# Narrow experts multiply the loaded float32 weights as they are, two products side by side in the halves of the array's columns

## The chip, the cores and the metric

The kernel runs on one core of one Trainium2 chip, as one program. The metric is the device time of an execution in microseconds. TensorE (PE; PEld are its weight loads) multiplies into PSUM, VectorE (DVE) and ScalarE (ACT) work between PSUM and SBUF, and SyncE (SP) issues nearly all transfers from memory.

## The reference

A network of four layers for 256 tokens and a width of 1024, in float32: a retention layer with a dense feed-forward part, a banded attention layer with a mixture of experts, and two layers of a second kind with a feed-forward part of 4096. The change touches only the mixture of experts:

```python
logits = (xn @ w_router).astype(jnp.float32)
top_v, top_i = lax.top_k(logits, 2)
top_w = jax.nn.softmax(top_v, axis=-1)
gates = jnp.sum(one_hot(top_i, 8) * top_w[..., None], axis=-2)
for e in range(8):
    y = y + gates[..., e:e + 1] * ((silu(xn @ w_gate[e]) * (xn @ w_up[e])) @ w_down[e])
```

Here w_gate and w_up are 1024 x 3584 for each expert and w_down is 3584 x 1024.

## The kernel before, in words

**Split products.** A float32 operand is split into a high part (ScalarE rounds it to the type fp32r) and a low part (VectorE subtracts the high part from the operand). A full product is three fp32r products: high x high, high x low and low x high (mm3, lines 343 to 345).

**The stream of weights.** All weights lie packed in the order of their use, in chunks of 128 partitions x 2048 numbers (1 MiB). The class Stream loads them with one transfer each, in that order, into places: 4 in the pool raw, 3 and 4 more in raw3 and raw4 that widen adds late in the attention layer for the time of the experts. _split makes the two parts of half a chunk (whi on line 288, wlo on line 289), and get asks for splits up to 5 half chunks ahead (HL). When the second half is split the place is free, and fill issues the next transfer into it (line 267).

**Turns of experts.** After the routing, the experts are put in an order by how many tokens chose them, and are worked on in eight turns. WIDE says which turns have 128 slots for tokens and which have 64: turns 1, 4 and 7 are narrow. gather picks the tokens of an expert by a product with a one-hot matrix oh and splits them. A wide turn has them as xgh and xgl and uses mm3. In a narrow turn the high part stands in the first 64 of 128 columns and the low part in the other 64, so that one product of 128 columns gives both; it is done with whi and with wlo (lines 1033 and 1034), and the two halves of the result have to be added.

**One step.** An expert has 14 steps j of 256 hidden columns. A step has two up chunks, with gate and up columns (8 blocks of 128 rows, 512 columns), and one down chunk (2 blocks of 128 rows, 1024 columns). In a narrow turn ScalarE copies the 512 result columns from PSUM (cp, line 1064), four products with the matrix fold (line 1069) turn them and add the two halves, ScalarE makes the silu (sgn, line 1073), VectorE multiplies (line 1074), and the result hh is split (lines 348 and 349) for the down products, which add to two PSUM banks acc. The down products of step j - 1 come after the up products of step j. At the end acc is split into yh and yl, a product with the one-hot matrix ohT brings the rows back to their tokens (line 1112), and VectorE adds them to h by their gates (line 1114).

**Order.** The planner of the language orders each engine's instructions by priority and by when they become ready in its own model; each engine then runs them in that order. Waits are derived from what is read and written. A wide turn has 24 up and 12 down products per step, a narrow one 16 and 8, and four with fold.

Of the kernel before, what the change touches and what calls it, by code (L numbers as in the profile page):

```python
# [227 lines left out]
class Stream:  # L228


    def __init__(self, prog, plans, raw_bufs, hl_bufs, raw_pool, hl_pool):
        self.nc = prog.nc
        self.items, self.parts, self.first = [], [], []
        for ap, plan in plans:
            offs, _ = offsets(plan)
            for c, o in zip(plan, offs):
                self.first.append(len(self.parts))
                step = max(c.kt // 2, 1)
                self.parts += [(len(self.items), k, step) for k in range(0, c.kt, step)]
# [3 lines left out]
        self.free = {raw_pool: raw_bufs}  # L243
        self.base, self.extra = raw_pool, []
# [4 lines left out]
    def widen(self, pool, bufs, until):  # L249

        self.extra.append(pool)
        self.free[pool] = bufs
        self.last = next(i for i, it in enumerate(self.items) if it[1].key == until)
        self.fill()

    def fill(self, most=None):
        while self.n_raw < min(len(self.items), most or len(self.items)):
            pool = next((p for p in self.extra if self.n_raw <= self.last and self.free[p]), self.base)
            if not self.free[pool]:
                return  # L260
            ap, c, o = self.items[self.n_raw]
            f = c.kt * c.n
            t = pool.tile([P, 2048], F32, name="wraw")
            if c.key[0] in ("eu", "ed"):
                e = self.expert[c.key[1]] if c.key[1] else 0
                src = ap[e:e + 1] if isinstance(e, int) else ap[bass.ds(e, 1)]
                self.nc.sync.dma_start(t[:, :f], src[:, o:o + P * f].rearrange("o (p f) -> (o p) f", p=P))
            else:
                step = f if self.n_raw else f // 2
                for c0 in range(0, f, step):  # L270
                    self.nc.sync.dma_start(t[:, c0:c0 + step],
                                           bass.AP(tensor=ap.tensor, offset=ap.offset + o + c0, ap=[[f, P], [1, step]]))
            self.free[pool] -= 1
            self.raw[self.n_raw] = t, pool
            self.n_raw += 1

    def _split(self):
        i, k, nk = self.parts[self.n_hl]
        c = self.items[i][1]
        self.fill()  # L280
        t, pool = self.raw[i]
        f = nk * c.n
        hi, lo = (self.hl_pool.tile([P, 1024], F32R, name=n) for n in ("whi", "wlo"))
        n = 1 if c.key[0] in ("eu", "ed") and c.key[1] < NE - 1 else 2
        for i0 in range(0, f, f // n):
            h, l = (x[:, i0:i0 + f // n] for x in (hi, lo))
            src = t[:, k * c.n + i0:k * c.n + i0 + f // n]
            self.nc.scalar.activation(h, src, AF.Copy)  # L288
            self.nc.vector.tensor_tensor(l, src, h.bitcast(F32), op=ALU.subtract)  # L289
        if k + nk == c.kt:  # L290
            self.free[pool] += 1
            del self.raw[i]
        self.hl[self.n_hl] = [x[:, :f].rearrange("p (k n) -> p k n", n=c.n) for x in (hi, lo)]
        self.n_hl += 1
        self.fill()

    def get(self, *keys):

        at = self.first[self.n_get]
# [3 lines left out]
        end = self.first[self.n_get]  # L303
        while self.n_hl < min(max(end, at + self.hl_bufs), len(self.parts)):
            self._split()
        return [[x[:, k, :] for x in self.hl[i]] for i in range(at, end) for k in range(self.parts[i][2])]


class Program:
# [200 lines left out]
    def run(self):  # L510
        nc, io = self.nc, self.io
        self.we = io["we"].rearrange("(e f) -> e f", e=NE)
        with ExitStack() as st, ExitStack() as self.later, \
                ExitStack() as self.routed, ExitStack() as self.wide:
            pool = self.lasting = lambda *a, **kw: st.enter_context(self.pool(*a, **kw))
            raw_pool, hl_pool = pool("raw", self.RAW), pool("hl", self.HL)
# [6 lines left out]
                            raw_pool, hl_pool)  # L523
# [279 lines left out]
    def widen(self, name, bufs):  # L803

        self.w.widen(self.wide.enter_context(self.pool(name, bufs)), bufs, ("ed", NE - 1, FFE // 256 - 1))
# [171 lines left out]
    def gather(self, px, pool, slot, turns, wide):  # L977
# [12 lines left out]
        xg = (px.tile([P, KD, n, P], F32R, name="xgh"), px.tile([P, KD, n, P], F32R, name="xgl"))  # L990
        for k2 in range(KD // 2):
            ks = slice(2 * k2, 2 * k2 + 2)
            ps = self.bank("ps")[:, :2 * n * P].rearrange("p (k e s) -> p k e s", k=2, e=n)
            for k in range(2):
                at = 0
                for x in self.xn:
                    for b in range(NB):
                        nc.tensor.matmul(ps[:, k], x[:, b, (2 * k2 + k) * P:(2 * k2 + k + 1) * P],
                                         oh[:, b], start=at == 0, stop=at == 3)
                        at += 1  # L1000
# [3 lines left out]
            flat = lambda t: t.rearrange("p k e s -> p k (e s)")  # L1004
            cut = nw * P + 64
            nc.scalar.activation(flat(xg[0][:, ks])[:, :, :cut], flat(ps)[:, :, :cut], AF.Copy)
            if nw:
                nc.vector.tensor_tensor(xg[1][:, ks, 0], ps[:, :, 0], xg[0][:, ks, 0].bitcast(F32), op=ALU.subtract)
            nc.vector.tensor_tensor(xg[0][:, ks, nw, 64:], ps[:, :, nw, 64:], xg[0][:, ks, nw, :64].bitcast(F32), op=ALU.subtract)
# [6 lines left out]
        return {i: ([x[:, :, a] for x in (xg if wide[i] else xg[:1])], ohT[:, a]) for a, i in enumerate(turns)}  # L1016

    def experts(self, px, pool, gates, slot, w, first, wide):
# [5 lines left out]
        for e in range(NE):  # L1024
            xg, ohT = have[e]
            acc = [self.bank("acc") for _ in range(2)]
            hT = {}

            def product(out, x, wk, start, stop):
                if wide[e]:  # L1030
                    self.mm3(out, x, wk, start, stop)
# [8 lines left out]
            def down(rows, by_half=False):  # L1040
                order = [(n, r) for n in range(2) for r in rows] if by_half else [(n, r) for r in rows for n in range(2)]
                for n, (j, k, wk) in order:
                    product(acc[n], [a[:, k, :] for a in hT[j]], [a[:, n * 512:(n + 1) * 512] for a in wk],
                            j == 0 and k == 0, j == nj - 1 and k == 1)

            def turned(j, ps):


                hh = pool.tile([P, 2, P], F32R, name="hh", bufs=2)
                if wide[e]:  # L1050
                    sg = self.work.tile([P, 256], F32, name="sg", tag="xs", bufs=3)
# [10 lines left out]
                hT[j] = (hh,)  # L1062
                cp = self.work.tile([P, 512], F32, name="cp", tag="xs", bufs=3)
                nc.scalar.activation(cp, ps, AF.Copy)

                def turn():
                    tp = self.bank("tp")[:, :256].rearrange("p (c s) -> p c s", s=64)
                    for c in range(4):
                        nc.tensor.matmul(tp[:, c], cp[:, c * P:(c + 1) * P], self.fold, start=True, stop=True)

                    def split():
                        sg = self.work.tile([P, 2, 64], F32, name="sgn", tag="xs", bufs=3)
                        nc.scalar.activation(sg, tp[:, :2], AF.Silu)
                        nc.vector.tensor_tensor(sg, sg, tp[:, 2:], op=ALU.mult)
                        self.split_psum(hh[:, :, :64], hh[:, :, 64:], sg)
# [4 lines left out]
            for j in range(nj):  # L1080
                ps = self.bank("mm")
                for k0 in (0, 4):
# [4 lines left out]
                    for k in range(4):  # L1087
                        product(ps, [a[:, k0 + k, :] for a in xg], wu[k],
                                k0 + k == 0, k0 + k == KD - 1)
# [13 lines left out]
            with self.tc.high_priority(offset=300) if e == NE - 1 else nullcontext():  # L1103
                for n in range(2):
                    spare = n and e == NE - 1
                    y = (pool.tile([P, 512], F32R, name="yh", bufs=2),
                         px.tile([P, 512], F32R, name="yl", tag="xgl") if spare else pool.tile([P, 512], F32R, name="yl"))
                    self.split_psum(*y, acc[n])
                    for b in range(NB):
                        ps = self.bank("ps")  # L1110
                        for i in range(2):
                            nc.tensor.matmul(ps, ohT[:, b * P:(b + 1) * P], y[i], start=i == 0, stop=i == 1)
                        s = self.h[:, b, n * 512:(n + 1) * 512]
                        nc.vector.scalar_tensor_tensor(s, ps, gates[:, b, e:e + 1], s, op0=ALU.mult, op1=ALU.add)

    def moe_layer(self):
# [19 lines left out]
        with tc.If(most > P):  # L1136
            with self.pool("moe2") as pool, self.pool("raw2", 2) as raw, \
# [495 lines left out]
```

## Time and profile before

| | us |
|---|---|
| median of 3 runs (2431.17 to 2432.93) | 2431.45 |
| profiled execution | 2430.9 |
| its span | 2429.1 |

The mean granted TensorE clock is 0.993 of full speed. The span is the time from the first to the last instruction in the trace. Busy times of TensorE are those of overlapping, pipelined products, so the distance between the starts of two products says more than a product's duration.

### The profile page before, as it was taken

What the parts mean: (1) busy time and instruction counts of PE and PEld (TensorE: products, weight loads), DVE (VectorE), ACT (ScalarE), POOL (GpSimd) and SP (SyncE); (2) the same over time, 40 slices, a digit from 0 to 9 for tenths busy, and PEclk for the clock granted to TensorE, in tenths of its full rate; (3) what the DMA queues carried; (4) which work ended last, traced back from release to release, by engine and by line L of the source; (5) the groups of instructions that cost most, each with busy time, mean ns of one, the idle gap of its engine ahead of it and who ended that gap; (6) DMA issues with size and microseconds to landing.
All of it is one profiled execution on the core that took longest, in us unless ns stands there. A gap on an engine that the chain in (4) does not pass through costs nothing. (4 is left out here: it accounts for less than half of the span.)

```text
span 2429.1 us, 35661 instructions
## 1 busy us (share of the span) xinstructions
PE 2372.9 (98%) x13033; PEld 1968.2 (81%) x13033; DVE 1891.5 (78%) x3027; ACT 1568.7 (65%) x2609; POOL 60.5 (2%) x105
## 2 busy tenths in 40 slices
PE   8999999999999999999999999899999999999999
PEld 7978998888876787876788876698789889878898
DVE  6756567778989989899998899778775567877655
ACT  6446555667878777778777789645755554575554
POOL 0000000000000000000000000100000000100000
PEclk9999999999999999999999999899999999999999
DMA  7445555567989998999999999534345554434552
GB/s 289 169 161 209 190 191 191 203 239 283 368 327 399 360 366 330 356 356 413 345 366 345 367 359 381 148 134 160 137 165 203 188 168 145 169 128 173 191 191 105
DMA packets 88121, 605.20 MB, mean 249 GB/s; under 512 B 10456, under 2 KB 12128, under 8 KB 17024
## 3 DMA queue, kind: packets, MB, share of 16 engines
q1 hardware_dynamic: 85520, 593.39, 65.5%
q0 software_dynamic: 2416, 9.44, 1.8%
q8 instruction: 104, 1.70, 0.3%
q14 instruction: 81, 0.66, 0.1%
HBM read 601.74 MB, written 1.05 MB: 248 GB/s over the span
## 5 line engine op out<-in xcount | busy, mean ns | idle before, releaser
L289 DVE TENSOR_TENSOR wlo<-wraw,whi 128x512 fp32r<-128x512 f32 (+1 forms) x1656 | 1383.5, 876 | 369.6 <-ACT whi L288 351.7
L288 ACT ACTIVATE whi<-wraw 128x512 fp32r<-128x512 f32 (+1 forms) x1656 | 1204.1, 776 | 437.0 <-PE mm L344 191.6
L343 PE MATMUL mm<-xth,whi 128*128 128x256 f32 x1296 | 364.0, 281 | 0.0
L345 PE MATMUL mm<-xth,wlo 128*128 128x256 f32 x1296 | 361.7, 279 | 1.5 <-DVE wlo L289 1.5
L344 PE MATMUL mm<-xtl,whi 128*128 128x256 f32 x1296 | 361.8, 279 | 0.0
L344 PEld LDWEIGHTS mm<-xtl,whi 128*128 128x128 f32 x1296 | 245.5, 189 | 3.9 <-issue 2.1
L343 PEld LDWEIGHTS mm<-xth,whi 128*128 128x128 f32 x1296 | 243.5, 188 | 5.2 <-issue 3.0
L344 PE MATMUL acc<-wlo,hh 128*128 128x512 f32 x624 | 247.2, 396 | 0.0
L345 PE MATMUL acc<-whi,hl 128*128 128x512 f32 x624 | 246.6, 396 | 0.0
L345 PEld LDWEIGHTS mm<-xth,wlo 128*128 128x128 f32 x1296 | 243.6, 188 | 2.4 <-DVE wlo L289 1.7
L343 PE MATMUL acc<-whi,hh 128*128 128x512 f32 x624 | 235.3, 397 | 1.3 <-ACT hh L348 1.3
L343 PE MATMUL mm<-whi,xth 128*128 128x512 f32 (+2 forms) x592 | 231.3, 391 | 2.0 <-ACT whi L288 2.0
L344 PE MATMUL mm<-wlo,xth 128*128 128x512 f32 (+2 forms) x592 | 231.5, 391 | 0.3 <-DVE wlo L289 0.3
L345 PE MATMUL mm<-whi,xtl 128*128 128x512 f32 (+2 forms) x592 | 229.6, 388 | 0.5 <-DVE xtl L349 0.5
L343 PE MATMUL mm<-whi,xgh 128*128 128x512 f32 x560 | 224.9, 402 | 2.7 <-ACT whi L288 2.6
L344 PE MATMUL mm<-wlo,xgh 128*128 128x512 f32 x560 | 223.0, 398 | 3.1 <-DVE wlo L289 3.0
L345 PE MATMUL mm<-whi,xgl 128*128 128x512 f32 x560 | 221.4, 395 | 0.0
L1034 PE MATMUL mm<-wlo,xgh 128*128 128x512 f32 x336 | 143.3, 427 | 5.4 <-DVE wlo L289 4.5
L343 PEld LDWEIGHTS acc<-whi,hh 128*128 128x128 f32 x624 | 117.5, 188 | 28.9 <-ACT hh L348 3.2
L345 PEld LDWEIGHTS acc<-whi,hl 128*128 128x128 f32 x624 | 117.3, 188 | 28.2 <-DVE hl L349 0.5
L344 PEld LDWEIGHTS acc<-wlo,hh 128*128 128x128 f32 x624 | 117.4, 188 | 26.4 <-DVE wlo L289 0.3
L1033 PE MATMUL mm<-whi,xgh 128*128 128x512 f32 x336 | 134.2, 400 | 0.0
(394 smaller groups left out, 3098.0 us busy)
## 6 DMA issues: line engine op xcount, KB each, us to landing
wraw<-in_we_dram SPq DMA_DIRECT2D x336, 1024.0 KB, 6.1
wraw<-in_w_dram SPq DMA_DIRECT2D x218, 1024.0 KB, 4.8
wraw<-in_w_dram SPq DMA_DIRECT2D x4, 912.0 KB, 4.6
wraw<-in_w_dram SPq DMA_DIRECT2D x6, 512.0 KB, 3.6
bias<-in_rel_rows_dram POOLq DMA_DIRECT2D x4, 768.0 KB, 4.6
gain<-in_norm_ffn_dram POOLq DMA_DIRECT2D x2, 512.0 KB, 7.1
gn<-in_ret_gn_dram SPq DMA_DIRECT2D x4, 256.0 KB, 3.8
gain<-in_norm_ple_dram POOLq DMA_DIRECT2D x2, 512.0 KB, 5.9
```

Of the source, the lines that this page charges most:

```text
L288: self.nc.scalar.activation(h, src, AF.Copy)
L289: self.nc.vector.tensor_tensor(l, src, h.bitcast(F32), op=ALU.subtract)
L343: mm(out, l[0], r[0], start=start, stop=False)
L344: mm(out, l[0], r[1], start=False, stop=False)
L345: mm(out, l[1], r[0], start=False, stop=stop)
L1033: nc.tensor.matmul(out, x[0], wk[0], start=start, stop=False)
L1034: nc.tensor.matmul(out, x[0], wk[1], start=False, stop=stop)
```

## The change

Stream takes a list of plain turns (1, 4 and 7). Their chunks get no parts: get hands out the loaded float32 numbers themselves, keeps the chunk in held, and frees its place at the next get. The places are now parts of one tile per pool (4, 3 and 4 places), handed out in the order in which they become free. Splits ahead are only asked for if the chunk's transfer has been issued.

gather makes xn, the 64 slots of a narrow expert in full float32, in place of the two parts side by side. The new helper halves multiplies 64 slots by two column halves of a weight block, into partitions 0 to 63 and 64 to 127 of one PSUM bank, one product after the other in program order. The up result is 256 columns wide (gate in the upper half, up in the lower half), two transposes take the place of the fold products, and the product of silu and up goes to hn in float32 with no split. The down result fits one bank; its rows are brought back to the tokens by products over 64 rows each.

```diff
     def get(self, *keys):
+        for i in self.held:
+            self.release(i)
...
+        while self.n_hl < min(max(end, at + self.hl_bufs), len(self.parts)) \
+                and (self.n_hl < end or self.parts[self.n_hl][0] in self.raw):
             self._split()
+        if not self.plain(self.items[start][1]):
+            return [[x[:, k, :] for x in self.hl[i]] for i in range(at, end) for k in range(self.parts[i][2])]
+        self.held = list(range(start, self.n_get))
+        return [[t[:, a, k * c.n:(k + 1) * c.n]] for i in self.held
+                for (t, a), c in [(self.raw[i], self.items[i][1])] for k in range(c.kt)]
...
+    def room(self, pool, n, last):
+        t = pool.tile([P, n, 2048], F32, name="wraw")
+        self.last[id(t)] = last
+        self.free += [(t, k) for k in range(n)]
...
+    def halves(self, out, xs, ws, first, last):
+        m, width = None, out.shape[1]
+        for i, (x, (w,)) in enumerate(zip(xs, ws)):
+            for n in range(2):
+                before = [m] if m else []
+                m = self.nc.tensor.matmul(out[64 * n:64 * n + 64], x, w[:, n * width:(n + 1) * width],
+                                          start=first and i == 0, stop=last and i == len(xs) - 1)
+                self.after(m, before)
+        return m
...
-                    nc.tensor.matmul(out, x[0], wk[0], start=start, stop=False)
-                    nc.tensor.matmul(out, x[0], wk[1], start=False, stop=stop)
+                    self.halves(ps[:, :256], [xg[:, k0 + k, :] for k in range(4)], wu, k0 == 0, k0 + 4 == KD)
...
+                if not wide[e]:
+                    if rows:
+                        ends.append(self.halves(acc[0], [hT[j][:, k, :] for j, k, _ in rows], [wk for *_, wk in rows],
+                                                 rows[0][:2] == (0, 0), rows[-1][:2] == (nj - 1, 1)))
+                    return
...
-                cp = self.work.tile([P, 512], F32, name="cp", tag="xs", bufs=3)
-                nc.scalar.activation(cp, ps, AF.Copy)
+                hT[j] = pool.tile([P, 2, 64], F32, name="hn", tag="hh", bufs=2)
+                cp = self.work.tile([P, 256], F32, name="cp", tag="xs", bufs=3)
+                nc.scalar.activation(cp, ps[:, :256], AF.Copy)
...
-                    for c in range(4):
-                        nc.tensor.matmul(tp[:, c], cp[:, c * P:(c + 1) * P], self.fold, start=True, stop=True)
+                    for k in range(2):
+                        self.after(nc.tensor.transpose(tp[:, k], cp[:, k * P:(k + 1) * P], self.ident), ends[-1:])
...
-                        self.split_psum(hh[:, :, :64], hh[:, :, 64:], sg)
+                        nc.vector.tensor_tensor(hT[j], sg, tp[:, :, 64:], op=ALU.mult)
```

## Rows read from the trace of the kernel before

**Rows 1.** The page: busy time, share and instructions of each engine.
```profile
PE 2372.9 (98%) x13033; PEld 1968.2 (81%) x13033; DVE 1891.5 (78%) x3027; ACT 1568.7 (65%) x2609; POOL 60.5 (2%) x105
```
**Rows 2.** Busy time by stretch: three narrow turns (1, 4, 7) and wide turn 5.
```profile
core 0: us, PE busy (x) PEld busy (x) DVE busy (x) ACT busy (x) POOL busy (x), PEclk, DMA share, GB/s
687.00:799.00 112.00, 100.64 (x460) 76.34 (x458) 104.63 (x116) 94.79 (x127) 0.00 (x0) 0.98 0.94 372
1054.00:1166.00 112.00, 106.40 (x487) 76.26 (x485) 107.18 (x119) 96.38 (x130) 0.00 (x0) 1.00 0.98 391
1166.00:1293.00 127.00, 125.58 (x548) 100.83 (x549) 114.08 (x125) 94.69 (x119) 0.00 (x0) 0.99 0.93 352
1416.00:1533.00 117.00, 110.75 (x472) 73.28 (x470) 116.16 (x213) 106.65 (x221) 0.00 (x0) 0.99 0.84 330
```
**Rows 3.** Waits from 1090 to 1160, in turn 4: total, times, longest.
```profile
PEld mm L1034 <- DVE wlo L289: 12.3, 27, 0.8
```
**Rows 4.** The same stretch, waits of the transfer queue alone.
```profile
SPq L267 <- DVE hh L349: 21.7, 10, 2.3
SPq L267 <- DVE sgn L1074: 19.3, 9, 2.2
SPq L267 <- DVE wlo L289: 17.9, 9, 2.6
```
**Rows 5.** The same stretch, instructions by line and shape: count | busy, mean ns.
```profile
L289 DVE TENSOR_TENSOR wlo<-wraw,whi 128x1024 fp32r<-128x1024 f32 x56 | 66.1, 1221 | 2.1 <-ACT whi L288 1.9
L288 ACT ACTIVATE whi<-wraw 128x1024 fp32r<-128x1024 f32 x56 | 55.9, 1049 | 0.0
...
L1064 ACT ACTIVATE cp<-mm 128x512 f32<-128x512 f32 x9 | 5.4, 597 | 3.3 <-PE mm L1034 3.3
...
L1074 DVE TENSOR_TENSOR sgn<-sgn,tp 128x128 f32<-128x128 f32 x9 | 2.5, 280 | 0.0
L1073 ACT ACTIVATE sgn<-tp 128x128 f32<-128x128 f32 x9 | 2.5, 279 | 3.5 <-PE tp L1069 3.5
```
**Rows 6.** Timeline of TensorE, first up products of two steps: start, duration.
```profile
1101.64 0.48 PE L1033 MATMUL mm<-whi,xgh 128*128 128x512 f32 x1
...
1109.18 0.48 PE L1033 MATMUL mm<-whi,xgh 128*128 128x512 f32 x1
```
**Rows 7.** Busy time by stretch: the steady parts of turns 4 and 5.
```profile
1100.00:1150.00 50.00, 48.73 (x219) 34.27 (x218) 48.83 (x54) 44.45 (x61) 0.00 (x0) 1.00 1.01 419
...
1200.00:1250.00 50.00, 50.00 (x224) 40.39 (x223) 43.62 (x47) 37.59 (x47) 0.00 (x0) 1.00 0.98 364
```
**Rows 8.** Timeline of TensorE: float32 products over all columns, and what follows.
```profile
1719.14 0.46 PE L1443 MATMUL sb<-sa,c_later 128*128 128x128 f32 x2 [0.20 <-DVE sa L1440]
...
1720.78 0.39 PE L1446 MATMUL sb<-sa,c_later 128*128 128x128 f32 x2
1720.92 0.47 PE L343 MATMUL mm<-whi,xth 128*128 128x512 f32 x1
```
**Rows 9.** Timeline of TensorE: float32 products in halves of the columns.
```profile
1723.31 0.88 PE L1453 MATMUL sb<-sa,sv 128*64 128x128 f32 x12
1724.12 0.50 PE L345 MATMUL mm<-whi,xtl 128*128 128x512 f32 x1
```
**Rows 10.** Timeline of TensorE: float32 transposes.
```profile
681.08 0.60 PE L1013 MATMUL tp<-ident,oh 128*128 128x128 f32 x4
681.43 0.48 PE L343 MATMUL acc<-whi,hh 128*128 128x512 f32 x1
```
**Rows 11.** Expert chunks issued before turn 1: count, size, median us to landing.
```profile
wraw<-in_we_dram SPq DMA_DIRECT2D x53, 1024.0 KB, 4.9
```
**Rows 12.** Timeline of TensorE, end of turn 7: its last down product.
```profile
1532.72 0.40 PE L1034 MATMUL acc<-wlo,hh 128*128 128x512 f32 x1
```
**Rows 13.** Waits from 566 to 686, in turn 0: total, times, longest.
```profile
ACT whi L288 <- DMA wraw<-in_we_dram: 7.4, 23, 0.3
```

More of the change, by code (lines that the diff above doesn't have):

```diff
@@ L237, in __init__ @@
                 self.first.append(len(self.parts))
-                step = max(c.kt // 2, 1)
-                self.parts += [(len(self.items), k, step) for k in range(0, c.kt, step)]
+                if not self.plain(c):
+                    step = max(c.kt // 2, 1)
+                    self.parts += [(len(self.items), k, step) for k in range(0, c.kt, step)]
                 self.items.append((ap, c, o))
@@ L242, in __init__ @@
         self.first.append(len(self.parts))
-        self.free = {raw_pool: raw_bufs}
-        self.base, self.extra = raw_pool, []
+        self.free, self.last, self.held = [], {}, []
         self.hl_pool, self.hl_bufs = hl_pool, hl_bufs
@@ L247, in __init__, with widen @@
         self.n_raw = self.n_hl = self.n_get = 0
[L249 to L253, printed above, removed]
+        self.room(raw_pool, raw_bufs, len(self.items))
+    def room(self, pool, n, last):
+        t = pool.tile([P, n, 2048], F32, name="wraw")
+        self.last[id(t)] = last
+        self.free += [(t, k) for k in range(n)]
+    def widen(self, pool, n, until):
+        self.room(pool, n, 1 + next(i for i, it in enumerate(self.items) if it[1].key == until))
         self.fill()
@@ L257, in fill @@
         while self.n_raw < min(len(self.items), most or len(self.items)):
-            pool = next((p for p in self.extra if self.n_raw <= self.last and self.free[p]), self.base)
-            if not self.free[pool]:
+            place = next((p for p in self.free if self.n_raw < self.last[id(p[0])]), None)
+            if place is None:
                 return
+            self.free.remove(place)
+            t, at = place
             ap, c, o = self.items[self.n_raw]
             f = c.kt * c.n
-            t = pool.tile([P, 2048], F32, name="wraw")
             if c.key[0] in ("eu", "ed"):
@@ L270, in fill, with release @@
                 for c0 in range(0, f, step):
-                    self.nc.sync.dma_start(t[:, c0:c0 + step],
+                    self.nc.sync.dma_start(t[:, at, c0:c0 + step],
                                            bass.AP(tensor=ap.tensor, offset=ap.offset + o + c0, ap=[[f, P], [1, step]]))
-            self.free[pool] -= 1
-            self.raw[self.n_raw] = t, pool
+            self.raw[self.n_raw] = place
             self.n_raw += 1
+    def release(self, i):
+        self.free.append(self.raw.pop(i))
+        self.fill()
     def _split(self):
@@ L280, in _split @@
         self.fill()
[L281 removed]
+        t, at = self.raw[i]
         f = nk * c.n
@@ L302, in get @@
             self.n_get += 1
-        end = self.first[self.n_get]
-        while self.n_hl < min(max(end, at + self.hl_bufs), len(self.parts)):
+        at, end = self.first[start], self.first[self.n_get]
+        self.fill()
+        while self.n_hl < min(max(end, at + self.hl_bufs), len(self.parts)) \
+                and (self.n_hl < end or self.parts[self.n_hl][0] in self.raw):
             self._split()
-        return [[x[:, k, :] for x in self.hl[i]] for i in range(at, end) for k in range(self.parts[i][2])]
+        if not self.plain(self.items[start][1]):
[3 more added lines that the diff above has]
+                for (t, a), c in [(self.raw[i], self.items[i][1])] for k in range(c.kt)]
 class Program:
@@ L522, in run @@
                                    (io["w2"], plan_second())], self.RAW, self.HL,
-                            raw_pool, hl_pool)
+                            raw_pool, hl_pool, [i for i in range(NE) if not WIDE[i]])
             self.h = self.keep.tile([P, NB, D], F32, name="h")
@@ L1025, in experts, with up @@
             xg, ohT = have[e]
-            acc = [self.bank("acc") for _ in range(2)]
-            hT = {}
-            def product(out, x, wk, start, stop):
+            acc = [self.bank("acc") for _ in range(2 if wide[e] else 1)]
+            hT, ends = {}, []
+            def up(ps, k0, wu):
                 if wide[e]:
-                    self.mm3(out, x, wk, start, stop)
-                else:
-                    nc.tensor.matmul(out, x[0], wk[0], start=start, stop=False)
-                    nc.tensor.matmul(out, x[0], wk[1], start=False, stop=stop)
+                    for k in range(4):
+                        self.mm3(ps, [a[:, k0 + k, :] for a in xg], wu[k], k0 + k == 0, k0 + k == KD - 1)
+                else:
+                    self.halves(ps[:, :256], [xg[:, k0 + k, :] for k in range(4)], wu, k0 == 0, k0 + 4 == KD)
             def rows_of(*js):
@@ L1086, in experts @@
                         split = None
-                    for k in range(4):
-                        product(ps, [a[:, k0 + k, :] for a in xg], wu[k],
-                                k0 + k == 0, k0 + k == KD - 1)
+                    up(ps, k0, wu)
                 rows = rows_of(j - 1) if 0 < j < nj - 1 else []
@@ L1103, in experts, with put_back @@
             with self.tc.high_priority(offset=300) if e == NE - 1 else nullcontext():
[L1104 to L1108, printed above, removed]
-                    for b in range(NB):
-                        ps = self.bank("ps")
-                        for i in range(2):
-                            nc.tensor.matmul(ps, ohT[:, b * P:(b + 1) * P], y[i], start=i == 0, stop=i == 1)
-                        s = self.h[:, b, n * 512:(n + 1) * 512]
-                        nc.vector.scalar_tensor_tensor(s, ps, gates[:, b, e:e + 1], s, op0=ALU.mult, op1=ALU.add)
+                def put_back(b, n, ps):
+                    s = self.h[:, b, n * 512:(n + 1) * 512]
+                    nc.vector.scalar_tensor_tensor(s, ps, gates[:, b, e:e + 1], s, op0=ALU.mult, op1=ALU.add)
+                for half, a in enumerate(acc):
+                    y = (pool.tile([P, 512], F32R, name="yh", bufs=2), pool.tile([P, 512], F32R, name="yl"))
+                    self.split_psum(*y, a)
+                    for b in range(NB):
+                        if wide[e]:
+                            ps = self.bank("ps")
+                            for i in range(2):
+                                nc.tensor.matmul(ps, ohT[:, b * P:(b + 1) * P], y[i], start=i == 0, stop=i == 1)
+                            put_back(b, half, ps)
+                            continue
+                        banks = [self.bank("ps") for _ in range(2)]
+                        last = None
+                        for i in range(2):
+                            for n in range(2):
+                                r = slice(64 * n, 64 * n + 64)
+                                m = nc.tensor.matmul(banks[n], ohT[r, b * P:(b + 1) * P], y[i][r], start=i == 0, stop=i == 1)
+                                self.after(m, [last] if last else [])
+                                last = m
+                        for n in range(2):
+                            put_back(b, n, banks[n])
     def moe_layer(self):
```

58 lines of the change are left out of this document (30 added, 28 removed).

## The prediction

> **What bounds the kernel now.** Start with the busy line of the page [rows 1]: TensorE is busy for 98% of the span, so at first sight only fewer or shorter products can help. That share is an average, so next cut the mixture-of-experts stage at the first up product of each expert. In the three narrow turns [rows 2] VectorE is busy for 107.18 of 112 us in the second one, TensorE shows pauses, and the transfers run faster than in the wide turn shown with them (391 against 352 GB/s). The waits of a quiet stretch of the second narrow turn say which of the three is late: the matrix engine waits for VectorE's low parts of the weights, 27 times, 12.3 us [rows 3], and nearly all the time of the transfer queue is waiting for VectorE too, because a buffer is free only when its low part is made: 21.7 + 19.3 + 17.9 = 58.9 of 70 us [rows 4]. So a narrow turn is bound by VectorE. One step j (256 of an expert's 3584 hidden columns, three chunks of 1 MiB) has six low parts of 1.221 us and two small operations of 0.28 us [rows 5], about 7.9 us with the small gaps of records overlapping; its period is 7.54 us, from 1101.64 to 1109.18 [rows 6].
>
> Behind VectorE stands the transfer, and close: in the steady part of a narrow turn it moves 419 GB/s at a share of 1.01 [rows 7]. A chunk is 1.0486 MB, so 2.50 us each and 7.50 us per j, 0.04 us below the period. In a wide turn it moves 364 GB/s while TensorE is busy for 50 of 50 us: there TensorE sets the pace and the queue has time to spare.
>
> **What the change removes.** In turns 1, 4 and 7 the 84 splits of each turn go: 84 x 1.221 = 103 us of VectorE and 84 x 1.049 = 88 us of ScalarE [rows 5]. Of the small work of a j the copy out of PSUM is half as wide (0.597 us at 512 columns), the product with the gate stays, and the split of hh goes. After it VectorE has one operation of about 0.28 us per j, and is out of the way.
>
> **What TensorE then needs per j.** Full float32 products stand in the trace, with 128 columns: 16 records (each product leaves two) start from 1719.14 on, and the next work starts at 1720.92 [rows 8]. That is 1.78 / 16 = 0.111 us for 128 columns, so 0.222 us for 256 and 0.445 us for 512. Products in halves of the columns stand there as well, with 128 columns: 12 records from 1723.31 to the next start at 1724.12, 0.81 us [rows 9]. One after another they would take 12 x 0.111 = 1.33 us; side by side 6 x 0.111 = 0.67 us. So the halves do run side by side, and 0.81 - 0.67 = 0.14 us is left for going into this form and out of it. A j of a narrow expert is then 8 pairs of up products, 8 x 2 x 0.222 = 3.55 us; 2 pairs of down products, 2 x 2 x 0.445 = 1.78 us; two transposes in place of the four fold products, by four transposes in 681.43 - 681.08 = 0.35 us [rows 10] 0.18 us; and once 0.14 us. Sum 5.65 us. The bounds of the pair: 1.0 of a full product's records (side by side), 2.0 (one after another), and 0.81 / 0.67 = 1.21 if the whole rest is a toll on each pair. I take 1.0, since the trace has this very form, with different moving data in both halves; 1.21 makes a j 6.8 us and stays in the range. The Trainium skill ("TensorE: Matmul & The Clock Gate", Measured speedup vs the span model) gives 2.38 for three column tiles, 0.79 of the ideal, which speaks against a full doubling; estimated from that page, a pair would cost 1.26 and the program come out near 2395. By that rule the 12 records would have taken 0.84 us, and the trace has 0.81 us with both changes of form in it, so this case can't fully tell the two apart.
>
> 14 x 5.65 = 79.1 us, and beside its 14 steps a narrow turn has 112 - 14 x 7.54 = 6.4 us today (first and last step, sums into h). I keep these: TensorE's side of a turn is 85.5 us. The chain behind a step (copy, transposes, 0.28 us of silu [rows 5], product) is under 2 us and lies beside the next step's 3.55 us of up products.
>
> **What the transfers then need.** 7.50 us per j is more than 5.65 us, so the ring of buffers decides. It has 11 places (4 + 3 + 4). When turn 1 begins, 53 chunks have been asked for and 42 are used up, so 11 are ahead [rows 11]; wide turns, at 2.85 us of TensorE per chunk against 2.50 us, fill it again: two of them win 84 x 0.35 = 29 us, 11 to 12 chunks. So 31 of a turn's 42 chunks must come during it. A narrow chunk now keeps its place until TensorE has read it: the first place is free after 8 x 0.222 = 1.8 us, its transfer lands 4.9 us later [rows 11], and the 42nd chunk lands 30 x 2.50 us after that, at 81.7 us. The first chunk of the next wide expert lands at 84.2 us, its first high part takes 1.05 us: the next turn begins at 85.3 us. Both sides meet at 85 to 86 us; where two limits are this close each adds a little waiting, so I take 88 us for turns 1 and 4, 24 us less than 112 each.
>
> Turn 7 today takes 117 us to its last down product, from 1416 to 1532.72 [rows 2, 12]; its splits are in halves. After: the 42nd chunk at 81.7 us, 1.8 us of products, and the last step's chain in between: 87 us, 30 us less.
>
> What becomes late: a wide turn after a narrow one starts with an empty ring, and its first splits wait for landings. Between 0 (transfers are faster than TensorE there) and 6 us (two landings) each for turns 2 and 5; I take 2.5 us each. The other edits cost nothing that shows: the gather's products have 192 in place of 256 columns, few and short; the sums into h are as many as before, after one split in place of two; the places of the ring are parts of one tile, which the queue waits for one by one as before. If instead a write waited for readers of other places, the queue would run with less ahead; bounds 0 to 8 us per turn, and I take 0, as the h tile is read and written in parts today.
>
> Sum, against the profiled execution of 2430.9 us (span 2429.1): -24 - 24 - 30 + 5 = -73, 2358 us. The median of the runs is 2431.45, within 0.6 us of it.
>
> The Trainium skill ("DMA: Bandwidth & Descriptors", Where 436 GB/s comes from) puts the limit of one core's share of HBM at about 358 GB/s. Estimated from that page a chunk would take 2.93 us, a narrow turn about 98 us, and the program about 2389 us; the trace holds 419 GB/s for 50 us [rows 7], so the measurement decides here.
>
> **Rivals.**
> - *A split for the next wide expert stands in the way.* ScalarE is in order. The splits look five parts ahead in the list of split chunks, and narrow chunks are not in it, so the first parts of the next wide expert can be placed on ScalarE as soon as their transfer has been issued, ten chunks early. If they stand ahead of the narrow steps' copies, TensorE waits at step 11 for the third wide chunk, at 81.7 + 3 x 2.50 = 89 us, and then has two steps and the end to do: 89 + 2 x 5.65 + 6.4 = 107 us. Gains of 5, 5 and 10 us less the 5 us after: about 2415, and 2400 where only part is delayed. For it: the code allows it. Against it: the planner orders by readiness; in turn 0 ScalarE waited for a transfer 23 times, but 0.3 us at most [rows 13].
> - *The ring gives nothing.* If it were empty at entry, a step would go from 7.54 to 7.50 us: 3 x 14 x 0.04 = 1.7 us, 2429. Against it are the 11 chunks ahead [rows 11].
> - *Pairs cost 1.21.* A turn is 14 x 6.8 + 6.4 = 101.6 us: -10, -10, -15, +0: 2396.
> - *Halves one after another (slower).* With 256 or 512 columns the two halves might not overlap, for their two float32 streams come from the same place. A j would be 2 x (3.55 + 1.78) + 0.32 = 10.98 us, a turn 160 us: +48 +48 +43, 2570 us. The change loses from a j of 7.54 us on, where a pair costs (7.54 - 0.32) / 5.33 = 1.35 of one product. Against it is the trace's pairing [rows 9], though at 128 columns.
> - *The change doesn't free VectorE* would be the case if splits of wide chunks filled the gap; these are the same number as before and only move earlier.
>
> **How the numbers follow.** Forecast 0.63, own range 2340 to 2380 (ends: the waiting of 2.7 us per turn and the wide starts at nothing and 5 us less at the end of turn 7; and 7 us per turn more). Late split 0.12; pairs at a toll 0.09; empty ring 0.04; serial halves 0.08; faster than 2340 0.04. The range from 2336 to 2414 takes in the forecast and most of two rivals, some 0.82. A change below 0.2% (4.9 us) can't be told from none. Faster: 0.63 + 0.12 + 0.09 + 0.04 = 0.88; within 0.04; slower 0.08.
>
> **What would show it.** In the profile after: no whi and wlo in the narrow turns but for the next expert's; pairs of 128*64 records with 256 columns 0.22 us apart (0.44 would be the serial rival); step period near 5.65 us in the first eight steps of a turn, and 7.5 us or waits for the transfers behind that; 419 GB/s through a narrow turn and on into the wide one; turns of 85 to 90 us. A pause of over 10 us at step 11, with ScalarE waiting for a transfer, would show the late split. The prediction is wrong if the period of the first steps is over 6.3 us, if the wide turns grow by over 5 us, or if the transfers stay below 400 GB/s in a narrow turn.

## The result, and the profile after

The changed kernel takes 2397.43 us (median of 4 runs, 2396.36 to 2398.46) against 2431.31 us (2430.47 to 2432.93) for the kernel before beside it: a ratio of 0.9858, 95% interval 0.9846 to 0.987. That is 34 us faster. The forecast of 2358 us had the direction right and more than double the gain; the time lies inside the range.

Where the time went, by the first up product of each turn in the two traces (turn 7: to its last down product; behind it: to a product of the next stage, at 1707.45 us before and 1672.31 after):

```
turn              before   after   change   forecast
1 (narrow)        112.8     94.7   -18.1     -24
2 (wide)          126.2    135.2    +9.0      +2.5
3 (wide)          128.7    125.4    -3.3       0
4 (narrow)        111.9     96.0   -15.9     -24
5 (wide)          126.9    134.6    +7.7      +2.5
6 (wide)          122.5    122.5     0         0
7 (narrow)        117.1     91.2   -25.9     -30
behind turn 7     174.7    186.1   +11.4       0
sum                                -35.1     -73
```

The span went from 2429.1 to 2394.6 us, -34.5; the table differs from it by the 0.6 us that the rest of the program behind its last row grew (turn 1 begins at 686.60 us in both traces). So about half of the miss lies in narrow turns that shrank less than forecast (18.1 us), and the other half in what follows them (23.1 us); turn 3 won 3.3 us that nobody forecast. The page's busy line, answering [rows 1]:

```profile
PE 2329.9 (97%) x13453; PEld 1879.8 (79%) x13453; DVE 1590.5 (66%) x2646; ACT 1300.9 (54%) x2224; POOL 61.5 (3%) x105
```

VectorE and ScalarE gave up 301 and 268 us, as three turns without splits should. Busy time by stretch, answering [rows 2 and 7]: turns 1, 2, 4, 5 and 7, then the steady part of turn 1.

```profile
core 0: us, PE busy (x) PEld busy (x) DVE busy (x) ACT busy (x) POOL busy (x), PEclk, DMA share, GB/s
686.60:781.30 94.70, 89.48 (x614) 46.23 (x613) 9.24 (x22) 12.68 (x34) 0.00 (x0) 1.00 0.87 355
781.30:916.50 135.20, 127.20 (x562) 101.07 (x561) 111.70 (x120) 92.64 (x117) 0.00 (x0) 0.97 0.93 384
1041.90:1137.90 96.00, 92.58 (x645) 48.66 (x644) 11.99 (x28) 15.22 (x38) 0.00 (x0) 1.00 0.90 363
1137.90:1272.50 134.60, 128.69 (x538) 100.76 (x537) 112.34 (x118) 91.92 (x114) 0.00 (x0) 0.94 0.95 392
1395.00:1486.60 91.60, 88.29 (x609) 45.87 (x608) 8.55 (x21) 10.85 (x31) 0.00 (x0) 1.00 0.95 387
712.00:748.00 36.00, 36.00 (x268) 18.88 (x266) 1.72 (x6) 4.35 (x13) 0.00 (x0) 1.00 1.01 420
```

VectorE's share in a narrow turn fell from 107 of 112 us to 12 of 96. In the steady part TensorE is busy throughout, and the transfers run at 420 GB/s with a share of 1.01, as before. TensorE's timeline there shows one step:

```profile
714.98 3.67 PE L1048 MATMUL mm<-wraw,xn 128*64 128x256 f32 x32
718.49 1.89 PE L1048 MATMUL acc<-wraw,hn 128*64 128x512 f32 x8
720.31 0.44 PE L1108 MATMUL tp<-ident,cp 128*128 128x128 f32 x2
720.67 3.67 PE L1048 MATMUL mm<-wraw,xn 128*64 128x256 f32 x32
```

From one set of up products to the next it is 720.67 - 714.98 = 5.69 us; the prediction worked out 5.65. The up products take 3.51 us (3.55 predicted), the down products 1.82 (1.78), the transposes with the change of form 0.36 (0.32).

Now the wide turn's beginning, which grew most. The waits of the transfer queue from 755 to 800 us (total, times, longest):

```profile
SPq L275 <- DMA wraw<-in_we_dram: 29.6, 5, 19.7
SPq L275 <- DVE wlo L300: 8.5, 2, 5.1
```

One wait lasts 19.7 us, for a landing, and then there are waits for low parts that are made from what has landed. The DMA strip of the same 45 us (40 slices of 1.125 us) shows what that does to the transfers:

```profile
DMA  9999999999999999999610000007970000048999
GB/s 393 459 408 408 422 444 415 415 401 437 415 408 415 430 437 415 401 444 415 262 66 0 0 0 0 0 0 167 444 306 29 0 0 0 0 58 306 393 422 466
```

At about 778 us the transfers stop. One chunk crosses near 787 us, and only from about 795 on is the stream there again. ScalarE, on its timeline, waits for that one chunk, and TensorE for ScalarE:

```profile
779.96 2.00 ACT L299 ACTIVATE whi<-wraw 128x1024 fp32r<-128x1024 f32 x2
790.60 2.00 ACT L299 ACTIVATE whi<-wraw 128x1024 fp32r<-128x1024 f32 x2 [8.64 <-DMA wraw<-in_we_dram]
```
```profile
791.71 0.80 PE L362 MATMUL mm<-whi,xw 128*128 128x512 f32 x1 [3.18 <-ACT whi L299]
```

The first step of turn 2 takes 18.68 us from up product to up product and the second 11.17, where a later step takes 8.53. In turn 5 they take 17.36 and 11.23 us. There the granted clock falls too, after TensorE had waited: to 0.50, the lower of its two levels (1.2 GHz), for 10 us.

```profile
1148.00:1158.00 10.00, 7.19 (x16) 4.51 (x16) 3.85 (x6) 4.46 (x6) 0.00 (x0) 0.50 0.86 342
```

The code says why. During a narrow turn, `get` looks five parts ahead in the list of split chunks, and that list has no narrow chunks; so the next parts in it are the next wide expert's. (A part is half a chunk, the piece that one split makes.) As soon as a wide chunk has been asked for, its splits are placed, and with the second of them its place is given back and handed, in program order, to the next chunk. That next transfer now waits for a chunk that has itself not yet landed, and for its split. The queue issues in order, so everything behind it waits too, while places that narrow products have long read stand empty. The trace's single transfers bear this out. From 759.07 us on none is asked for until 784.42, and the next comes at 794.08: these two wait for a landing and for VectorE. Ahead of them, from 695 to 755 us, no wait of the queue for a landing is over 2.2 us. Behind 794.08 seven more are asked for within 4.1 us, as their places had long been free.

### The profile page after: what moved, and what is told of

The parts are those of the page before. It is cut to its first block, busy times and chain, and to the rows that moved or that the text cites. A ratio compares the mean times of both kernels' runs of the same rounds, so it can differ in the third digit from the quotient of the medians.

```text
span 2394.6 us, 35474 instructions
## 1 busy us (share of the span) xinstructions
PE 2329.9 (97%) x13453; PEld 1879.8 (79%) x13453; DVE 1590.5 (66%) x2646; ACT 1300.9 (54%) x2224; POOL 61.5 (3%) x105
## 5 line engine op out<-in xcount | busy, mean ns | idle before, releaser
L300 DVE TENSOR_TENSOR wlo<-wraw,whi 128x512 fp32r<-128x512 f32 (+2 forms) x1320 | 1080.9, 855 | 374.5 <-ACT whi L299 355.2
L299 ACT ACTIVATE whi<-wraw 128x512 fp32r<-128x512 f32 (+2 forms) x1320 | 942.1, 760 | 445.6 <-PE mm L363 197.3
L1048 PE MATMUL mm<-wraw,xn 128*64 128x256 f32 x1344 | 161.4, 383 | 3.1 <-DMA wraw<-in_we_dram 3.1
L1113 DVE TENSOR_TENSOR hn<-sgn,tp 128x128 f32<-128x128 f32 x42 | 12.1, 287 | 222.6 <-ACT sgn L1112 222.6
L362 PE MATMUL mm<-whi,xgh 128*128 128x512 f32 x336 | 136.7, 407 | 2.7 <-ACT whi L299 2.7
L1048 PEld LDWEIGHTS mm<-wraw,xn 128*64 128x64 f32 x1344 | 93.8, 137 | 56.9 <-issue 10.4
L363 PE MATMUL mm<-wlo,xgh 128*128 128x512 f32 x336 | 135.8, 404 | 1.8 <-DVE wlo L300 1.8
```

Of the source, the lines that this page charges most:

```text
L362: mm(out, l[0], r[0], start=start, stop=False)
L363: mm(out, l[0], r[1], start=False, stop=False)
L1048: m = self.nc.tensor.matmul(out[64 * n:64 * n + 64], x, w[:, n * width:(n + 1) * width], start=first and i == 0, stop=last and i == len(xs ...
L1113: nc.vector.tensor_tensor(hT[j], sg, tp[:, :, 64:], op=ALU.mult)
```

## Experiments

Theory P is this: places handed on ahead of a landing stop the queue. Its rival R: the transfers' rate, with an empty ring behind each narrow turn, is what the wide turns pay for. The kernel before, run beside the first four, took 2431.96 us (median, 2429.82 to 2432.97), and beside the last four 2432.73 (2429.6 to 2435.88).

**No splits ahead in a narrow turn.** The look-ahead is off while the current expert is narrow.

```diff
+        ahead = 0 if self.plain(self.items[start][1]) else self.hl_bufs
-        while self.n_hl < min(max(end, at + self.hl_bufs), len(self.parts)) \
+        while self.n_hl < min(max(end, at + ahead), len(self.parts)) \
```

> The changed kernel with one edit: while a narrow expert asks for its chunks, no split of the next wide expert's chunks is asked for ahead. Theory P (places): in the changed kernel those early splits hand the place of the newest chunk to the next transfer; the transfer queue is in order and stands still for 25 us until that chunk has landed and is split, so the wide turns 2 and 5 start late (135.2 and 134.6 us against 126.2 and 126.9 before) and so does the stage behind turn 7. Without them the gap between the issues of the next wide expert's first and second chunk falls from 25 us to under 4 us, turns 2 and 5 take 126 to 129 us, and the program 2365 to 2380 us. Rival R (rate): the ring is empty after a narrow turn and 2.5 us per chunk sets the wide start anyhow; the edit changes less than 4 us: 2393 to 2400 us.

Measured: 2371.66 us (2368.63 to 2374.25), ratio 0.9754 (0.9737 to 0.977), 26 us below the changed kernel. Turns 2 to 5 by stretch, without turn 3, which stayed as it was:

```profile
781.70:907.00 125.30, 124.09 (x561) 99.91 (x560) 111.44 (x120) 92.53 (x117) 0.00 (x0) 0.99 1.01 415
1032.50:1129.90 97.40, 93.14 (x645) 48.59 (x644) 12.03 (x28) 15.23 (x38) 0.00 (x0) 1.00 0.96 392
1129.90:1253.40 123.50, 121.88 (x538) 96.90 (x537) 111.83 (x118) 91.83 (x114) 0.00 (x0) 1.00 1.01 413
```

The wide turns are 9.9 and 11.1 us shorter than in the changed kernel, with the DMA share up from 0.93 and 0.95 to 1.01 and the granted clock of turn 5 at 1.00 in place of 0.94. From turn 7's last down product on it wins 7.4 more. The queue's longest wait from 755 to 800 us is now 2.2 us:

```profile
SPq L275 <- DMA wraw<-in_we_dram: 34.2, 18, 2.2
```

Theory P holds, and R's 2393 to 2400 us is out.

**Splits ahead, but no place handed on.** This separates the two halves of P: the early splits stay on ScalarE, and only their places are kept back until the wide expert begins.

```diff
         if k + nk == c.kt:
-            self.release(i)
+            if self.narrow:
+                self.kept.append(i)
+            else:
+                self.release(i)
...
+        if not self.narrow:
+            for i in self.kept:
+                self.release(i)
+            self.kept = []
```

> The changed kernel with one edit: the early splits stay, but the places of chunks split during a narrow turn are handed back only when the wide expert asks for its first chunk. Theory P: the queue's order of places is what matters, not the splits on ScalarE, so this comes out within 4 us of the kernel without early splits, 2365 to 2382 us. If early splits standing in ScalarE's order were the cause, it would stay at 2393 to 2400 us while the kernel without early splits gets faster. Rival R: 2393 to 2400 us for both.

Measured: 2373.61 us (2371.14 to 2374.2), ratio 0.9762 (0.9746 to 0.9779), the same as without the splits (the two intervals overlap); turn 2 takes 125.7 us. So the early splits cost nothing on ScalarE that shows. The place handed on does.

**Half of each narrow chunk.** This takes away half of a narrow turn's traffic and leaves the look-ahead as in the changed kernel.

```diff
+                take = f // 2 if self.plain(c) else f
-                self.nc.sync.dma_start(t[:, at, :f], src[:, o:o + P * f].rearrange("o (p f) -> (o p) f", p=P))
+                self.nc.sync.dma_start(t[:, at, :take], src[:, o:o + P * f].rearrange("o (p f) -> (o p) f", p=P)[:, :take])
```

> The changed kernel, but each chunk of a narrow expert is loaded only in its first half (the second half of the place holds older numbers), so that a narrow turn needs half of its transfers; all else is as in the changed kernel. Rival R (the rate of the transfers sets narrow ends and wide starts): all waits for chunks go, narrow turns take 14 x 5.69 + 6 to 10 = 86 to 90 us against 94.7 and 96.0, wide turns 2 and 5 start as before, 2350 to 2362 us. Theory P: the narrow turns get shorter as well (about 5 us each), but the queue still stands still until the newest wide chunk is split, so turns 2 and 5 keep 3 us or more of their late start: 2365 to 2380 us.

Measured: 2362.52 us (2 runs, 2362.25 to 2362.79), ratio 0.9716 (0.9697 to 0.9735): 2.5 us below P's span and 0.5 us above R's. It doesn't separate the two: with less to load the newest chunk lands early, and the queue's longest wait for a landing from 745 to 800 us is 5.6 us in place of 19.7. Turn 2 takes 126.2 us with no other cure.

**Half after half.** All products of one half of the columns in a call, then all of the other.

```diff
-        for i, (x, (w,)) in enumerate(zip(xs, ws)):
-            for n in range(2):
+        for n in range(2):
+            for i, (x, (w,)) in enumerate(zip(xs, ws)):
```

> The changed kernel with the same products in another order: in each call first all products into the lower half, then all into the upper half, so that neighbours go to the same half and can't run beside each other. Theory (halves run side by side): a step goes from 5.69 us to 10 to 11 us, a narrow turn to 150 to 165 us, the program to 2560 to 2620 us. Rival (the gain came from the splits alone, a product of 64 slots is cheap in itself): a step under 6.5 us, under 2430 us.

Measured: 2431.97 us (1 run). The step is 6.71 us, and both expectations missed:

```profile
726.55 0.44 PE L1108 MATMUL tp<-ident,cp 128*128 128x128 f32 x2
726.91 4.05 PE L1048 MATMUL mm<-wraw,xn 128*64 128x256 f32 x29
...
731.45 1.88 PE L1048 MATMUL acc<-wraw,hn 128*64 128x512 f32 x6
733.26 0.44 PE L1108 MATMUL tp<-ident,cp 128*128 128x128 f32 x2
```

From the first up product to where down products run alone it is 731.45 - 726.91 = 4.54 us, with two of the eight down records inside, against 3.51 us for the up products side by side. So the halves overlap even when they are issued in blocks, and this order takes only a part of the pairing away; a sharper test follows.

**Both products of a pair in one half.** Only the first pair of each sum is left side by side; the upper half's columns of the result are left out.

```diff
-                m = self.nc.tensor.matmul(out[64 * n:64 * n + 64], x, w[:, n * width:(n + 1) * width],
-                                          start=first and i == 0, stop=last and i == len(xs) - 1)
+                own = first and i == 0
+                h = n if own else 0
+                m = self.nc.tensor.matmul(out[64 * h:64 * h + 64], x, w[:, n * width:(n + 1) * width],
+                                          start=own, stop=h == 1 or (last and i == len(xs) - 1 and n == 1))
```

> The changed kernel with both products of a pair in the lower half of the array's columns, save the first pair of each sum; the upper half's columns of the result are left out. Side by side is real: the two products now follow one another, a step j is 1 x 0.44 + 7 x 0.89 + 2 x 1.78 + 0.32, about 10.5 us, a narrow turn about 152 us, less the 28 us of standing queue that a longer turn hides: 2545 to 2575 us. Rival (the pairs' nearness in the records is the profiler's, and the halves share the array in time): the step stays at 5.7 to 6 us and the program at 2395 to 2410 us.

Measured: 2540.12 us (1 run). The step is 10.42 us:

```profile
711.10 6.69 PE L1050 MATMUL mm<-wraw,xn 128*64 128x256 f32 x32
717.62 3.60 PE L1050 MATMUL acc<-wraw,hn 128*64 128x512 f32 x8
721.15 0.44 PE L1110 MATMUL tp<-ident,cp 128*128 128x128 f32 x2
721.52 1.73 PE L1050 MATMUL mm<-wraw,xn 128*64 128x256 f32 x9
```

6.52 us of up products against 3.51, 3.53 us of down products against 1.82: the same products, one after another. Side by side is real, and a pair has the price of one product over all columns (3.51 us against the 3.55 worked out at 1.0). The time is 5 us below the expected span, as turn 1 came to 147.5 us and not 152.

**The ring alone.** The kernel before with the changed ring (places as parts of one tile) and every expert split, `plain` being empty:

```diff
+        t = pool.tile([P, n, 2048], F32, name="wraw")
+        self.free += [(t, k) for k in range(n)]
```

> The kernel before with the changed ring of buffers alone: places as parts of one tile, released as in the changed kernel, and every expert still split. Theory P (a place costs something only when it is handed on ahead of a landing, which needs a turn whose own chunks are not in the list of splits): no difference, 2427 to 2436 us. Rival R (parts of one tile make the queue wait for readers of other places): 2440 us or more, with the narrow turns' transfers below 380 GB/s.

Measured: 2431.37 us (2429.35 to 2435.65), ratio 0.9998 (0.9987 to 1.0008). The queue's waits from 1090 to 1160 us answer [rows 4] nearly number for number:

```profile
SPq L275 <- DVE hh L368: 19.4, 9, 2.2
SPq L275 <- DVE sgn L1093: 19.3, 9, 2.2
SPq L275 <- DVE wlo L300: 17.9, 9, 2.6
```

The ring's new form costs nothing. It costs in company with chunks that the look-ahead doesn't see.

**Half loads and no splits ahead.** Both edits together: what the rate of the transfers costs once the queue no longer stops. The edit is the first and the third diff.

> The changed kernel with no split ahead of a wide expert during a narrow turn, and with half of each narrow chunk loaded (the second half of its columns holds older numbers): what the rate of the transfers still costs once no place is handed on early. Theory T (narrow turns are then at TensorE's pace, and the next wide turn begins with a full ring): turns 1 and 4 take 84 to 87 us, turns 2 and 5 about 124 us, 2338 to 2354 us. Rival (the half loads and the missing stop were the same gain twice): 2359 to 2365 us, as half loads alone.

Measured: 2350.32 us (2 runs, 2348.83 to 2351.8), ratio 0.9663 (0.9644 to 0.9683), 21 us below the cure alone. Turns 1 and 4:

```profile
687.30:773.20 85.90, 85.43 (x602) 45.08 (x601) 13.95 (x25) 15.30 (x35) 0.00 (x0) 1.00 0.75 264
...
1025.70:1118.00 92.30, 91.10 (x638) 48.68 (x637) 17.78 (x32) 18.17 (x40) 0.00 (x0) 1.00 0.79 282
```

Turn 1 is at TensorE's own pace, 85.9 us with 85.4 busy. Turn 4 has 36 records more, the gather of the next experts' tokens (32) and four transposes, and takes 92.3, where 84 to 87 was expected. The wide turns missed their expectation of 124 us to both sides: turn 5 takes 121.5 us and turn 2 130.8, with a granted clock of 0.97. The clock fell at the end of turn 2, to 0.66 from 894 to 904 us, after TensorE had waited 1.7 us for VectorE in the gather; turns 2 and 3 together take 252.5 us, against 250.8 with the first cure alone.

**The first step early.** On top of the first cure, a narrow turn's first two calls of up products get precedence over the tail of the expert before, so that the first place comes free sooner.

```diff
-                    up(ps, k0, wu)
+                    with self.tc.high_priority(offset=300) if j == 0 and e and not wide[e] else nullcontext():
+                        up(ps, k0, wu)
```

> The changed kernel with no split ahead of a wide expert during a narrow turn, and with the products of a narrow turn's first step placed ahead of the tail of the expert before, so that the ring's first place is free some 9 us sooner. Theory F (what is left of the forecast's 88 us per narrow turn is the late first place, since the turn's last chunks arrive as much later): turns 1, 4 and 7 each lose 4 to 8 us, 2348 to 2362 us. Rival (TensorE's own work sets the end, or the tail's delay costs what the place gains): 2368 to 2376 us, as without the move.

Measured: 2375.0 us (2369.51 to 2376.34), ratio 0.9758 (0.9739 to 0.9776): no gain over the cure alone. The first transfer of turn 1 is indeed asked for at 686.97 us, in place of 695.24. But the tail that was pushed back then stands among the products of the next steps, whose places come later: the third transfer is asked for at 703.29 us, in place of 701.44. DMA from 676 to 712 us with the cure alone, then with the move:

```profile
676.00:688.00 12.00, 11.67 (x71) 10.06 (x69) 8.86 (x18) 5.98 (x11) 0.00 (x0) 1.00 0.77 308
688.00:700.00 12.00, 12.00 (x64) 6.77 (x64) 4.53 (x7) 1.96 (x4) 0.00 (x0) 1.00 0.27 93
700.00:712.00 12.00, 12.00 (x90) 6.36 (x92) 0.86 (x3) 1.60 (x5) 0.00 (x0) 1.00 0.96 395
```
```profile
676.00:688.00 12.00, 10.59 (x66) 8.23 (x64) 7.07 (x11) 5.31 (x9) 0.00 (x0) 1.00 0.86 320
688.00:700.00 12.00, 11.32 (x61) 7.68 (x62) 3.97 (x12) 3.11 (x7) 0.00 (x0) 1.00 0.48 171
700.00:712.00 12.00, 12.00 (x80) 6.08 (x78) 3.09 (x6) 1.04 (x3) 0.00 (x0) 1.00 0.64 240
```

In these 36 us 9.6 MB cross without the move (308 + 93 + 395, by 12 us each) and 8.8 MB with it. An early first place is worth nothing if the next ones are late.

## Where the prediction was right, and where it failed

The forecast was 73 us and the gain 34. The step that failed is the price of what becomes late behind a narrow turn: the prediction let an empty ring cost 2.5 us twice and nothing behind turn 7, and the hand-on of places cost 26 us of the program. The second, smaller step is the first free place, 1.8 us into a turn by the prediction and 7.1 us in the trace. The rest follows term by term.

**TensorE's step: right.** 5.69 us against 5.65. The pairing at 1.0 of a product, which decided against the rivals "toll" (6.8 us a step) and "one after another", is shown by the run in one half: 10.42 us there, 10.98 worked out. That the total falls on the toll's 2396 us is chance. One of the sums beside this term was off: with a pair at 1.26 the step is 1.26 x 5.33 + 0.32 = 7.04 us, a turn 104.9 us, and the program about 2405 us, not 2395. And the transfers of a narrow turn were not faster than those of turn 5 in all three: turn 7 moved 330 GB/s against 352 [rows 2].

**TensorE's side of a narrow turn: right for turn 1, short for turn 4.** 85.5 us was predicted; with half loads and no stop turn 1 takes 85.9. Turn 4 takes 92.3. The 6.4 us "beside its 14 steps" were carried over from the times of turns bound by VectorE, where TensorE's extra work of turn 4 didn't show. That work, the gather of the next experts, stood in the rows: 106.40 us of TensorE in turn 4 against 100.64 in turn 1 [rows 2].

**The turn's end by the transfers: mis-sized.** "The first place is free after 1.8 us" failed. TensorE in the changed kernel, from the turn's first product on:

```profile
686.60 1.08 PE L1048 MATMUL mm<-wraw,xn 128*64 128x256 f32 x6
687.60 0.51 PE L362 MATMUL acc<-whi,hh 128*128 128x512 f32 x1
...
691.56 1.08 PE L1048 MATMUL mm<-wraw,xn 128*64 128x256 f32 x6
692.57 0.50 PE L1151 MATMUL ps<-yh,ohT 128*128 128x512 f32 x1
693.00 1.08 PE L1048 MATMUL mm<-wraw,xn 128*64 128x256 f32 x6
```

Six of the first chunk's 16 records run, then the last down products of turn 0 and the products that bring its rows back to their tokens, and the 16th record stands in the group at 693.00. The first transfer of the turn is asked for at 693.70:

```profile
693.70 6.53 SPq L275 DMA_DIRECT2D wraw<-in_we_dram  x3
```

That is 7.1 us into the turn in place of 1.8. From there the prediction's own arithmetic, 30 more chunks at 2.50 us, puts the whole turn 5.3 us later: 85.3 + 5.3 = 90.6 us. The places behind the first are late as well. The turn's first transfer lands 4.8 us after it is asked for, at 698.5 us, and its 31st, the 42nd chunk, is asked for at 756.6 and lands 20.2 us later, at 776.8: 78.3 us for 30 chunks in place of 75.0. That makes 93.9 of the 94.7 us of turn 1; with the queue unblocked it takes 93.6, against 88. That the late places are the cause follows from these times; the attempt to move the first one didn't bring the gain, so their price isn't shown by a run of its own. What is shown is the sum: 21 us in the program for the whole chunks against the halves.

**The wide turns behind: the step that failed.** The prediction weighed the look-ahead only as a matter of ScalarE's order (the "late split", which would stop step 11 of the narrow turn), and of the ring it asked only whether parts of one tile would make the queue wait for other readers: "I take 0". Both answers were right, as the ring alone (2431.37 us) and the kept places (2373.61 us) show. What was not asked is which landing the next transfer in the queue waits for once the place that it gets belongs to a chunk still on its way. Turns 2 and 5 grew by 9.0 and 7.7 us, where an empty ring was given 2.5; over 5 us was the prediction's own sign of being wrong. Without the hand-on they are 9.9 and 11.1 us shorter than in the changed kernel, and 0.9 and 3.4 us shorter than before the change, so even the 2.5 us wasn't due.

**Behind turn 7: not in the sum at all.** The prediction ended turn 7 at its last down product. The next stage's weights are in the same list, their splits are asked for in the narrow turn as well, and the queue waits for landings there too: first the changed kernel from 1465 to 1530 us, then the kernel with the look-ahead off from 1446 to 1510.

```profile
SPq L279 <- DMA wraw<-in_w_dram: 12.2, 2, 8.2
SPq L279 <- DMA wraw<-in_we_dram: 7.0, 1, 7.0
```
```profile
SPq L279 <- DMA wraw<-in_we_dram: 6.2, 3, 2.1
```

The queue's waits for low parts don't tell the two apart: they are 21.0 us there in the changed kernel and 30.4 with the look-ahead off. A vector of norm gains is late too: VectorE waits for it, and TensorE behind that. First VectorE, then TensorE, in the changed kernel:

```profile
1505.68 1.23 DVE L1201 TENSOR_TENSOR gm<-gm,gf 128x1024 f32<-128x1024 f32 x1 [5.80 <-DMA gm<-in_norm_mix_dram]
```
```profile
1507.56 0.50 PE L364 MATMUL mm<-whi,xtl 128*128 128x512 f32 x1 [3.48 <-DVE xtl L368]
```

With the look-ahead off the first of these two waits, of 5.80 us here, is 1.53 us, and 7.4 of the 11.4 us come back. The other 4.0 us, and the 3.3 us that turn 3 won, were not traced.

In sum: of the 39 us between forecast and result the early hand-on of places accounts for 26 (shown by two runs). The rest is the narrow turns, which with the look-ahead off still take 93.6, 97.4 and 92.5 us where 88, 88 and 87 were forecast, less what the wide turns then win beyond the forecast. Their late places and turn 4's extra work account for that by the times of the trace, not by a run that changes these alone. With the look-ahead off the kernel beats both versions, at 2371.66 us.

## What to carry to other kernels

When part of a stream leaves a look-ahead list, ask what the list's next entry is now, and which buffer it gives back how early: in an in-order queue one transfer that waits for a fresh landing stops all those whose buffers are free. A turn that becomes bound by transfers grows by as much as its first free buffers are late, so look for what is interleaved with its first reads, and don't expect an early first buffer to help if the second isn't early as well. Take the fixed part of a stage from the engine that will bind it, not from the engine that binds it now.

## What the hardware showed that was not expected

Products in the two halves of the array's columns overlap without alternating in program order: with four products to one half and then four to the other, a step takes 6.71 us, nearer to side by side (5.69) than to one after another (10.42 with all but the first pairs in one half). One core also kept up 420 GB/s with 36 us of TensorE busy beside it, as in the kernel before.
